# Unsplit fp32 products for most chunks, both branch projections among them, and another order in the second block

## The chip, the cores and the metric

The kernel runs on one NeuronCore of a Trainium2 chip. The metric is device time in microseconds (us) from launch to end, as the median of several runs. The engines are TensorE (PE in the profile, with its weight loads as PEld), VectorE (DVE), ScalarE (ACT), GpSimd (POOL) and SyncE (SP, whose queue issues most of the loads). Work is bound together by semaphores; each engine executes its own list of instructions in order.

## The reference, cut to what matters

A sequence of 256 tokens with 1024 features goes through two blocks in fp32. The change touches the second block alone:

```python
h = _rmsnorm(x, norm_mix_g)
proj = h @ w_in                       # r, k, v, the conv's input (glu), two gates
rkv = rkv + (_token_shift(rkv) - rkv) * mu_rkv
a_out = _rwkv7_mixer(h, r, k, v, ...)     # recurrence over tokens, 16 heads of 64
c_out = _conformer_conv_mixer(glu_in, ...)  # u * sigmoid, 31-tap conv per feature, layer norm, silu
gates = sigmoid(gate_logits).reshape(b, t, 2, 1024)
merged = gates[:, :, 0] * (a_out @ w_rwkv_proj) + gates[:, :, 1] * (c_out @ w_conv_proj)
x = x + merged @ w_out
x = x + square(relu(_rmsnorm(x, norm_ff_g) @ w_ff1)) @ w_ff2
```

## The kernel before

Activations of the second block stand feature-first: eight tiles of 128 features by 256 tokens. Weights come from HBM in **chunks** of 512 output features, each chunk in four pieces of 512 KB (256 input features by 512 outputs). A piece is loaded into `raw` by the SP queue (`fetch`, a ring of three slots).

Most products are **split products** (`feat`, line 266). `split` (lines 238 and 239) makes two tiles of a piece: `whi`, rounded to the matmul's short fp32 form by ACT, and `wlo`, the remainder, by DVE. The activations have been split in the same way (`xh`, `xl`). A 128x128 weight block then takes three matmuls, hi by hi, hi by lo and lo by hi: 96 matmuls of 256 columns for a chunk. `whi` and `wlo` have three slots each (`streams("s2", 3, 3)`). The output projection and the feed-forward (`toks`, line 284, and `feat`) take the same slots. Only `gated` (line 1586, the projection of the conv branch) multiplies **unsplit** fp32 weights, 32 products for a chunk, straight from tiles `wd`, which it places in the slots of `whi` and `wlo`.

The string `PROG` lists the steps of the second block's middle: K and R are the r, k, v products of the first and second half of the heads (three chunks each), L the low-rank products, A the preparation of a half's recurrence (norms by a `rsqrt` of ten DVE instructions), B its block matrices `G` with a small triangular solve on DVE whose data go through HBM (`blka`, `sy`, `blkb`, `T0T`), M the five pipelined steps of a half's recurrence over its chunks of tokens (chains of 64x64 matmuls with evictions between them; each step depends on the last), O the normalisation of its output into `y`, U the conv's input (two chunks each, half of the features), C one feature tile of the 31-tap convolution (`conv_tile`, 30 DVE instructions of line 1454, called taps here, after one ACT instruction), G a chunk of gates, S the layer norm of the conv's output, D the `gated` projection of a chunk of the conv branch. `merge2` follows: it splits `y` into hi and lo, multiplies it by `w_rwp` as a split product, merges, and multiplies by `w_o2`.

A planner turns this list into one order for each engine: it takes the instructions that are ready and lets later steps fill the waits of earlier ones; a step marked "!" keeps its first matmul or tap at its place in the list. So a step's instructions stand mingled with those of its neighbours, and matmuls of a chunk that stand in a recurrence's chain are called fillers here.

Of the kernel before, what the change touches and what calls it, by code (L numbers as in the profile page):

```python
# [167 lines left out]
class Net:  # L168
# [87 lines left out]
    def feat(self, xh, xl, src, n=4, tag="A", pieces=None, pin=lambda i: None):  # L256

        nc = self.nc
        out = [self.bank((128, 256), tag) for _ in range(n)]
        for k0, kn, hi, lo in (self.pieces(src, 128 * n) if pieces is None else pieces):  # L260
            for f in range(n):
                c = slice(f * 128, f * 128 + 128)
                for k in range(kn):
                    kt = k0 + k
                    for j, (w, x) in enumerate(((hi, xh), (hi, xl), (lo, xh))):
                        pin(nc.tensor.matmul(out[f], w[:, k, c], x[:, kt, :], start=(kt == 0 and j == 0),  # L266
                                             stop=(kt == 7 and j == 2)))
        return out
# [78 lines left out]
    def diag(self, r, n=2):  # L347

        out = []
        for tt in range(n):  # L350
            d = self.tmp.tile([128, 128], F32, name=self.name("dg"), tag="dg", bufs=2)
            self.nc.vector.tensor_scalar(d, self.ident, r[:, tt:tt + 1], None, op0=ALU.mult)
            out.append(d)
        return out

    def transpose_chunk(self, X, c, xh, xl, wcol=None, dg=None):


        nc = self.nc
        for fp in range(2 * c, 2 * c + 2):  # L360
            ps = self.bank((128, 2, 256), "B")
            for f in range(2):
                ft = 2 * fp + f
                for tt in range(2):
                    o, x = ps[:, f, tt * 128:tt * 128 + 128], X[:, tt, ft * 128:ft * 128 + 128]
                    if dg is None:
                        nc.tensor.transpose(o, x, self.ident)
                    else:
                        nc.tensor.matmul(o, x, dg[tt], start=True, stop=True)
            if wcol is None:  # L370
# [678 lines left out]
    def ple(self):  # L1049
        nc, a = self.nc, self.a  # L1050
        V, PE, S = nc.vector, nc.tensor, nc.scalar
        X2 = self.X2
        xh, xl = self.a8(F32R, s="xh"), self.a8(F32R, s="xl")
        for c in range(2):
            self.transpose_chunk(X2, c, xh, xl, "plw")
        s2 = self.small((128, 2), s="s2")
        V.tensor_reduce(s2, self.ss2, axis=AX.X, op=ALU.add)
        r = self.rstd_of(s2)
        self.ple_proj()
        wrow = self.act.tile([128, 1024], F32, name="wrow2", tag="row")  # L1060
        nc.gpsimd.dma_start(wrow, a["rows"][0])

        xw = self.a8(shape=(128, 2, 1024), s="xw")
        sa = self.small((128, 2, 2, 2), s="sa")
        for c in range(2):
            s = slice(512 * c, 512 * c + 512)
            for tt, ps in enumerate(self.toks(xh, xl, a["w_pg"][c])):
                g = self.t2(s="g")
                S.activation(g, ps, AF.Sigmoid, scale=r[:, tt:tt + 1])
                V.tensor_mul(g, g, self.U[:, tt, s])  # L1070
                V.tensor_add(X2[:, tt, s], X2[:, tt, s], g)
                self.square_sum(X2[:, tt, s], sa[:, 0, tt, c:c + 1])
# [12 lines left out]
        for c in range(2):  # L1085
            self.transpose_chunk(xw, c, *self.x2, "mixw", dg)
        self.rsqrt(v1, r1, t)
        for tt in range(2):
            nc.gpsimd.tensor_scalar(xw[:, tt, :], xw[:, tt, :], r1[:, tt:tt + 1], 1.0, op0=ALU.mult, op1=ALU.mult)
        self.xs = nc.dram_tensor("x_mid", (128, 2, 1024), F32).ap()  # L1090
        nc.gpsimd.dma_start(self.xs, xw)
# [354 lines left out]
    def conv_tile(self, up, ft, pin):  # L1446
# [35 lines left out]
    def mix2(self, late):  # L1482
        nc, a = self.nc, self.a
        V, PE, S, G = nc.vector, nc.tensor, nc.scalar, nc.gpsimd
        keep = self.keep
        xh, xl = self.x2
        self.y = y = self.cst.tile([128, 8, 256], F32, name="y", tag="xp")
        up = keep.tile([128, 8, 286], F32, name="up")
        with self.work("wkv", 1, 1):
            gates = self.branches(xh, xl, y, up)  # L1490
        self.tap("y", y)
        x4 = late.enter_context(self.pool("x4", 1, side="right"))
        self.x4 = [x4.tile([128, 8, 256], F32R, name=m) for m in ("h4", "l4")]
        with self.pool("post") as post:
            self.merge2(y, gates, post)

    def branches(self, xh, xl, y, up):
        nc, a = self.nc, self.a
        V, G = nc.vector, nc.gpsimd
        self.const2 = self.act.tile([128, a["const2"].shape[1]], F32, name="const2", tag="const2")  # L1500
# [12 lines left out]
        k0, k1, gates, st = {}, {}, {}, [{}, {}]  # L1513
        for tok in PROG.split():
            pin = self.pin(tok.endswith("!"))
            op, arg = tok[0], [int(x) for x in tok[1:].rstrip("!")]
            n = arg[0] if arg else 0
            if op == "L":
                self.lor = self.loras(xh, xl)
            elif op == "K":  # L1520
                k0[n] = self.rkv(xh, xl, n, 0, pin)
            elif op == "R":
                k1[n] = self.rkv(xh, xl, n, 1, pin)
            elif op == "U":
                self.glu(xh, xl, up, n, pin)
            elif op == "C":
                self.conv_tile(up, n, pin)
            elif op == "G":
                gates[n] = self.gate(xh, xl, n, pin)
            elif op == "S":  # L1530
                self.conformer(up, pin)
            elif op == "D":
                self.gated(gates[2 + n], up[:, :, 30:286], a["w_cvp"][n], pin)
            else:
# [37 lines left out]
        for f, ps in enumerate(self.feat(xh, xl, a["w_glu"][c])):  # L1572
            V.tensor_mul(up[:, 4 * c + f, 30:286], ps, sg[:, f, :])

    def gated(self, gt, z, w, pin):

        nc = self.nc
        out = [self.bank((128, 256), "A") for _ in range(4)]
        for p in range(4):
            pool, tag = ((self.wsp, "whi"), (self.wsp, "wlo"))[p % 2]  # L1580
            r = pool.tile([128, 2, 512], F32, name=self.name("wd"), tag=tag)
            nc.sync.dma_start(r, w[p])
            for f in range(4):
                for k in range(2):
# [3 lines left out]
        for f in range(4):  # L1588
            nc.vector.tensor_mul(gt[:, f, :], out[f], gt[:, f, :])

    def merge2(self, y, gates, post):
        nc, a = self.nc, self.a
        V, S, G = nc.vector, nc.scalar, nc.gpsimd
        yh, yl, mh, ml = (post.tile([128, 8, 256], F32R, name=n) for n in ("yh", "yl", "mh2", "ml2"))
        self.split_act(y, yh, yl, V)
        for c in range(2):
            for f, ps in enumerate(self.feat(yh, yl, a["w_rwp"][c])):
                m = self.t2((128, 256), s="m")
                V.tensor_mul(m, ps, gates[c][:, f])
                V.tensor_add(m, m, gates[2 + c][:, f])  # L1600
                S.activation(mh[:, 4 * c + f, :], m, AF.Copy)
                V.tensor_sub(ml[:, 4 * c + f, :], m, mh[:, 4 * c + f, :].bitcast(F32))
# [69 lines left out]


PROG1 = "X0 X1 T Z0 Z1 W D0 D1 Y5 Y6 Y0 Y1 Y2 v1 r Y3 Y4 Y7 N q0 q1 R0 k0 S k1 R1 v0 B1 A0 P12 A1 A2 B0 A3 A4 A5 A6 A7 P6 C0 C1"
PROG = "K0 L K2 K1 A0 U0 B0 U1 M0 M0 M0 M0 M0 O0 R0 R1 R2 A1 G0 B1 G2 M1 M1 M1 M1 G1 G3 M1 C0 C1 C2 C3 C4 C5 C6 C7 O1 S D1 D0"
STEPS = "m0 p0,m1 p1 s0,m2 p2 s1,m3 p3 s2,s3"
NEARLY = 12
NFIRST = 38
# [3 lines left out]
def net(ctx, tc, a, off, tap=None, upto=99):  # L1682
# [9 lines left out]
                n.mix1()  # L1692
                n.moe()
    late = ctx.enter_context(ExitStack())
    with n.streams("s2", 3, 3):
        with n.pool("keep") as n.keep:
            n.x2 = [n.keep.tile([128, 8, 256], F32R, name=m, tag=m) for m in ("xh2", "xl2")]
            with n.work("p3", 5):
                n.ple()
            n.mix2(late)  # L1700
# [19 lines left out]
```

## Time and profile before

| | |
|---|---|
| median of 3 runs | 1257.74 us (1257.6 to 1259.7) |
| the profiled execution | 1260.09 us |
| its span | 1258.4 us |
| mean granted TensorE clock | 0.955 |
| PE busy | 1131.2 us, 90% of the span |
| DVE busy | 745.1 us, 59% |
| ACT busy | 511.5 us, 41% |

The second block's middle runs from about 621 us (first product of K0) to about 1043 us (end of the product with `w_rwp`); the output projection takes until about 1070 us, the feed-forward until about 1247 us. The shares above are means over very different stages, so the stretches are to be read one by one: how much of a stretch PE is busy, at which granted clock (1.00 is 2.4 GHz, 0.50 is 1.2 GHz, a mean in between is a mixture of the two), and how busy DVE is at the same time.

### The profile page before, as it was taken

What the parts mean: (1) busy time and instruction counts of PE and PEld (TensorE: products, weight loads), DVE (VectorE), ACT (ScalarE), POOL (GpSimd) and SP (SyncE); (2) the same over time, 40 slices, a digit from 0 to 9 for tenths busy, and PEclk for the clock granted to TensorE, in tenths of its full rate; (3) what the DMA queues carried; (4) which work ended last, traced back from release to release, by engine and by line L of the source; (5) the groups of instructions that cost most, each with busy time, mean ns of one, the idle gap of its engine ahead of it and who ended that gap; (6) DMA issues with size and microseconds to landing.
All of it is one profiled execution on the core that took longest, in us unless ns stands there. A gap on an engine that the chain in (4) does not pass through costs nothing.

```text
span 1258.4 us, 20687 instructions
## 1 busy us (share of the span) xinstructions
PE 1131.2 (90%) x8211; PEld 887.1 (70%) x8211; DVE 745.1 (59%) x1513; ACT 511.5 (41%) x881; POOL 119.7 (10%) x126
## 2 busy tenths in 40 slices
PE   5999999999979988878789899998749999999996
PEld 5988976667754433216687798887736797999995
DVE  4777677656532111106846799889884366656555
ACT  4643644544411000006536535556215335545453
POOL 0002330001000000000200501014200000000000
PEclk9999999999979999998889899998857999999998
DMA  8743555327769999994353365122420136555552
GB/s 300 277 162 104 155 179 167 120 98 288 272 258 409 409 409 409 409 408 146 116 184 132 98 183 157 52 93 84 150 60 2 35 108 233 179 189 191 189 187 99
DMA packets 82981, 242.26 MB, mean 193 GB/s; under 512 B 24160, under 2 KB 24416, under 8 KB 82496
## 3 DMA queue, kind: packets, MB, share of 16 engines
q1 hardware_dynamic: 80224, 231.11, 51.3%
q0 software_dynamic: 2224, 8.90, 2.6%
q8 instruction: 66, 1.08, 0.4%
q10 hardware_dynamic: 432, 0.89, 0.2%
q14 instruction: 35, 0.29, 0.1%
HBM read 234.31 MB, written 4.46 MB: 190 GB/s over the span
## 4 chain that ended last, share of the span: by engine, by line
PE 47%; DVE 11%; DMA 5%; ACT 3%; issue 2%; POOL 1%; DVEq 0%; ACTq 0%; POOLq 0%; SPq 0%
PE ps L266 17%; PE acc L284 7%; DVE cv L1454 4%; PE ps L986 3%; PE ps L1007 3%; DMA we<-in_w_gu 3%; PE ps L284 2%; DVE wlo L239 2%; PE ps L1586 2%; PE ps L955 2%; DMA we<-in_w_dn 2%; PE acc L1015 2%; PE ps L1304 1%; ACT whi L238 1%; PE ps L1045 1%
## 5 line engine op out<-in xcount | busy, mean ns | idle before, releaser
L239 DVE TENSOR_TENSOR wlo<-raw,whi 128x1024 fp32r<-128x1024 f32 (+1 forms) x230 | 291.7, 1272 | 157.9 <-ACT whi L238 155.9
L238 ACT ACTIVATE whi<-raw 128x1024 fp32r<-128x1024 f32 (+1 forms) x230 | 242.2, 1055 | 289.7 <-PE ps L266 141.4
L266 PE MATMUL ps<-xh,whi 128*128 128x256 f32 x760 | 222.7, 293 | 9.1 <-DVE rkv L1135 4.2
L266 PE MATMUL ps<-xh,wlo 128*128 128x256 f32 x760 | 219.6, 291 | 1.6 <-DVE wlo L239 1.6
L266 PE MATMUL ps<-xl,whi 128*128 128x256 f32 x760 | 220.8, 291 | 0.0
L266 PEld LDWEIGHTS ps<-xh,whi 128*128 128x128 f32 x760 | 149.2, 196 | 14.7 <-DVE rkv L1135 4.7
L266 PEld LDWEIGHTS ps<-xh,wlo 128*128 128x128 f32 x760 | 148.4, 196 | 4.6 <-issue 1.8
L266 PEld LDWEIGHTS ps<-xl,whi 128*128 128x128 f32 x760 | 149.4, 197 | 3.1 <-issue 2.3
L1454 DVE SCALAR_TENSOR_TENSOR cv<-up,par,cv 128x256 f32<-128x256 f32 x232 | 106.3, 498 | 0.6
L986 PE MATMUL ps<-we,xg 128*32 128x512 f32 x512 | 75.9, 597 | 4.8 <-DMA we<-in_w_gu 4.8
L266 PE MATMUL ps<-h,whi 128*128 128x256 f32 x256 | 72.2, 282 | 0.0
L266 PE MATMUL ps<-l,whi 128*128 128x256 f32 x256 | 71.9, 281 | 0.0
L266 PE MATMUL ps<-h,wlo 128*128 128x256 f32 x256 | 71.9, 281 | 0.0
L284 PE MATMUL ps<-wlo,xh 128*128 128x512 f32 x128 | 50.7, 397 | 1.8 <-DVE wlo L239 1.8
L284 PE MATMUL ps<-whi,xh 128*128 128x512 f32 x128 | 50.9, 398 | 0.0
L284 PE MATMUL ps<-whi,xl 128*128 128x512 f32 x128 | 50.5, 394 | 0.0
L284 PE MATMUL acc<-wlo,fh 128*128 128x512 f32 x128 | 49.9, 390 | 0.0
L284 PE MATMUL acc<-whi,fl 128*128 128x512 f32 x128 | 49.9, 390 | 0.0
L284 PE MATMUL acc<-whi,fh 128*128 128x512 f32 x128 | 49.8, 389 | 0.0
L1007 PE MATMUL ps<-we,gT 128*32 128x512 f32 x256 | 44.1, 600 | 6.2 <-DVE gT L1001 3.5
L986 PEld LDWEIGHTS ps<-we,xg 128*32 128x32 f32 x512 | 16.4, 109 | 46.6 <-issue 24.8
L266 PEld LDWEIGHTS ps<-h,whi 128*128 128x128 f32 x256 | 48.2, 188 | 0.6 <-ACT re L1634 0.2
(477 smaller groups left out, 2025.2 us busy)
## 6 DMA issues: line engine op xcount, KB each, us to landing
we<-in_w_gu SPq DMA_DIRECT2D x128, 512.0 KB, 10.2
we<-in_w_dn SPq DMA_DIRECT2D x64, 512.0 KB, 10.2
raw<-in_w_ff SPq DMA_DIRECT2D x64, 512.0 KB, 4.2
raw<-in_w_g SPq DMA_DIRECT2D x32, 512.0 KB, 3.2
raw<-in_w_qkv SPq DMA_DIRECT2D x24, 512.0 KB, 3.2
raw<-in_w_rkv SPq DMA_DIRECT2D x24, 512.0 KB, 3.3
raw<-in_w_o SPq DMA_DIRECT2D x16, 512.0 KB, 5.8
raw<-in_w_glu SPq DMA_DIRECT2D x16, 512.0 KB, 3.2
```

The costliest lines, as they stand in the source:

```text
L238: nc.scalar.activation(hi, r, AF.Copy)
L239: nc.vector.tensor_sub(lo, r, hi.bitcast(F32))
L266: pin(nc.tensor.matmul(out[f], w[:, k, c], x[:, kt, :], start=(kt == 0 and j == 0), stop=(kt == 7 and j == 2)))
L284: pin(nc.tensor.matmul(out[tt], x[:, x0 + k, s], w[:, k, :], start=(kt == 0 and j == 0), stop=(kt == last and j == 2)))
L955: PE.matmul(ps[:, f, :], X1[:, tt, ft * 128:ft * 128 + 128], Pm[:, tt, :], start=(tt == 0), stop=(tt == 1))
L986: PE.matmul(gu[32 * e:32 * e + 32, :], xg[:, kt, 32 * e:32 * e + 32], w[e // 2][:, e % 2, :], start=(kt == 0), stop=(kt == 7), skip_group_ ...
L1007: PE.matmul(py[h][32 * e:32 * e + 32, :], gT[:, kt * 128 + 32 * e:kt * 128 + 32 * e + 32], w[e // 2][:, e % 2, :], start=(kt == 0), stop=( ...
L1015: PE.matmul(acc[tt][h], PT[:, tt * 128:tt * 128 + 128], y, start=False, stop=(q == 7 and n == 1), skip_group_check=True)
L1045: PE.matmul(ps, x[:, kt, ts], ww[:, kt, :], start=(n == 0), stop=(n == 5))
L1304: PE.matmul(ps[H(h), q, :], lhs[H(h), q, :], r, start=True, stop=True)
L1454: pin(nc.vector.scalar_tensor_tensor(last, x[:, j:j + 256], self.P("cw", 8 * j + ft), o, op0=ALU.mult, op1=ALU.add))
L1586: pin(nc.tensor.matmul(out[f], r[:, k, 128 * f:128 * f + 128], z[:, kt, :], start=(kt == 0), stop=(kt == 7)))
```

## The change

1. `feat` gets a second form: with `xl=None` it takes the loaded pieces as they are and makes one fp32 matmul where the split form makes three. The new tokens with "f" use it with `x32`, an unsplit copy of the activations: R0, R1, R2, U0, U1 (two chunks each) and G0 to G3.
2. `transpose_chunk` writes `x32` too, by eight more ACT instructions at the end of the first block. It takes 8 KB of each partition, and `wsp` now has two slots each for `whi` and `wlo` instead of three.
3. The product with `w_rwp` leaves `merge2` and becomes the steps W0 and W1, made by `gated` with unsplit weights; `y` is no longer split.
4. `PROG` is another list: the second half's products R, and its A, come ahead of the first half's recurrence, U0 after them; conv tiles are placed between the steps of both recurrences; W0 and W1 stand around S, ahead of D0 and D1. `diag` gets a third slot. (`conv_sum`, a conv on PE, is defined but no token calls it.)

So 13 chunks change form: three R, four U, four G and two W. K0 to K2 and L stay split, as do `w_o2` and the feed-forward.

```diff
     def feat(self, xh, xl, src, n=4, tag="A", pieces=None, pin=lambda i: None):
...
         out = [self.bank((128, 256), tag) for _ in range(n)]
+        if xl is None:
+            for p in range(4):
+                r = self.fetch(src[p])
+                for f in range(n):
+                    for k in range(2):
+                        kt = 2 * p + k
+                        pin(nc.tensor.matmul(out[f], r[:, k, f * 128:f * 128 + 128], xh[:, kt, :], start=(kt == 0),
+                                             stop=(kt == 7)))
+            return out
...
+                if x32 is not None:
+                    nc.scalar.activation(x32[:, ft, :], ps[:, f, :], AF.Copy, scale=self.P(wcol, ft))
...
+            xs = (x32, None) if "f" in tok else (xh, xl)
...
+            elif op == "W":
+                self.gated(gates[n], y, a["w_rwp"][n], pin)
...
-        yh, yl, mh, ml = (post.tile([128, 8, 256], F32R, name=n) for n in ("yh", "yl", "mh2", "ml2"))
-        self.split_act(y, yh, yl, V)
+        mh, ml = (post.tile([128, 8, 256], F32R, name=n) for n in ("mh2", "ml2"))
         for c in range(2):
-            for f, ps in enumerate(self.feat(yh, yl, a["w_rwp"][c])):
-                m = self.t2((128, 256), s="m")
-                V.tensor_mul(m, ps, gates[c][:, f])
+            for f in range(4):
+                m = gates[c][:, f]
                 V.tensor_add(m, m, gates[2 + c][:, f])
...
-PROG = "K0 L K2 K1 A0 U0 B0 U1 M0 M0 M0 M0 M0 O0 R0 R1 R2 A1 G0 B1 G2 M1 M1 M1 M1 G1 G3 M1 C0 C1 C2 C3 C4 C5 C6 C7 O1 S D1 D0"
+PROG = "K0 K2 L K1 A0 R0f R1f R2f B0 A1 U0f M0 C0 M0 M0 C1 G1f M0 M0 B1 O0 C2 U1f M1 C3! G0f M1 C6 M1 G3f M1 M1 C4! G2f C5 C7! O1 W0 S W1 D0 D1"
...
-    with n.streams("s2", 3, 3):
+    with n.streams("s2", 3, 2):
```

How the order moves shows at three places. In the rows below a line number of the new kernel is 9 to 27 higher than that of the same statement before (266 became 275 for split products, 1304 became 1315, 1312 became 1323, 1454 became 1465, 377 became 386).

On PE, the second half's recurrence begins. Before:

```order
L1304 MATMUL ps_8111<-const_82,T0T 64x64 x8
L1304 MATMUL ps_8121<-T_1473_8105,LT_8104 64x64 x8
L1304 MATMUL ps_8131<-T_1474_8106,T0T 64x64 x8
L1304 MATMUL ps_8141<-T0T,T_1474_8106 64x64 x8
L1319 MATMUL ps_8151<-T_1476_8108,G_7871 32x32 x8
L1327 MATMUL ps_8162<-T_1475_8107,T_1474_8106 32x32
```

In the new kernel, at the same place, where line 266 is now the unsplit product (`x` is `x32`, and the weights are the raw tile):

```order
L1315 MATMUL ps_7447<-const_82,T0T 64x64 x8
L266 MATMUL ps_7580<-x_4807,raw_7602 128x256 x2
L1315 MATMUL ps_7457<-T_1395_7441,LT_7440 64x64 x8
L266 MATMUL ps_7581<-x_4807,raw_7602 128x256 x2
L1315 MATMUL ps_7467<-T_1396_7442,T0T 64x64 x8
L1315 MATMUL ps_7477<-T0T,T_1396_7442 64x64 x8
L266 MATMUL ps_7578<-x_4807,raw_7612 128x256
L1330 MATMUL ps_7487<-T_1398_7444,G_7109 32x32 x8
```

Gate products now stand between the links of the chain, where before link followed on link: 59 unsplit products are spread over this recurrence.

On DVE, the same recurrence; `cv` and the last `up` of a tile are the convolution's taps, `T` the chain's evictions, and "x16" is a run of sixteen. Before:

```order
L1454 SCALAR_TENSOR_TENSOR cv_9150<-up,par,cv_9150 128x256
L1454 SCALAR_TENSOR_TENSOR cv_9182<-up,par,cv_9182 128x256
L1454 SCALAR_TENSOR_TENSOR up<-up,par,cv_9150 128x256
L1454 SCALAR_TENSOR_TENSOR cv_9182<-up,par,cv_9182 128x256 x16
L1312 TENSOR_TENSOR T_1476_8108<-ps_8131,T_1473_8105 128x256
L1313 TENSOR_TENSOR T_1475_8107<-ps_8141,T0T 128x256
L1454 SCALAR_TENSOR_TENSOR cv_9182<-up,par,cv_9182 128x256 x4
L1454 SCALAR_TENSOR_TENSOR up<-up,par,cv_9182 128x256
L1466 TENSOR_SCALAR mean_9319<-ps_9310 128x256
```

In the new kernel:

```order
L1465 SCALAR_TENSOR_TENSOR cv_7763<-up,par,cv_7763 128x256
L1323 TENSOR_TENSOR T_1398_7444<-ps_7467,T_1395_7441 128x256
L1465 SCALAR_TENSOR_TENSOR cv_7763<-up,par,cv_7763 128x256
L1324 TENSOR_TENSOR T_1397_7443<-ps_7477,T0T 128x256
L1465 SCALAR_TENSOR_TENSOR cv_7545<-up,par,cv_7545 128x256
L1465 SCALAR_TENSOR_TENSOR cv_7763<-up,par,cv_7763 128x256
L1465 SCALAR_TENSOR_TENSOR cv_7545<-up,par,cv_7545 128x256
```

Before, the convolution is nearly over when the second recurrence begins. Now 86 of its 240 taps stand in the first recurrence, 101 in the second, and a run of 27 behind the second's last eviction.

On ACT, the end of the first block, where the activations of the second are written (`xh` and, in the new kernel, `x`, which is `x32`), and the first halves of weights after them. Before:

```order
L377 ACTIVATE xh_4805<-ps_5149,par 128x256
L377 ACTIVATE xh_4805<-ps_5140,par 128x256
L377 ACTIVATE xh_4805<-ps_5149,par 128x256
L238 ACTIVATE whi_5288<-raw_5286 128x1024
L238 ACTIVATE whi_5336<-wl_5330 128x1024
```

In the new kernel:

```order
L386 ACTIVATE xh_4805<-ps_5156,par 128x256
L390 ACTIVATE x_4807<-ps_5145,par 128x256
L390 ACTIVATE x_4807<-ps_5156,par 128x256
L386 ACTIVATE xh_4805<-ps_5156,par 128x256
L238 ACTIVATE whi_5267<-raw_5265 128x1024
L390 ACTIVATE x_4807<-ps_5156,par 128x256
L238 ACTIVATE whi_5297<-raw_5295 128x1024
L238 ACTIVATE whi_5341<-raw_5339 128x1024
```

The eight writes of `x32` stand between those of `xh`, one of them even behind the next piece's `whi`; and the pieces that follow are now K2's (`raw`), where L's scaled weights (`wl`) stood.

## Rows read from the trace of the kernel before

**Rows 1.** Part 1 of the page: busy time, share of the span, instructions of an engine.

```profile
PE 1131.2 (90%) x8211; PEld 887.1 (70%) x8211; DVE 745.1 (59%) x1513; ACT 511.5 (41%) x881; POOL 119.7 (10%) x126
```

**Rows 2.** Windows: length, busy (instructions) of PE, PEld, DVE, ACT, POOL; clock, DMA share, GB/s.

```profile
621.00:675.00 54.00, 49.79 (x390) 49.35 (x389) 29.96 (x50) 24.11 (x36) 8.75 (x11) 0.94 0.56 183
675.00:711.00 36.00, 29.08 (x184) 22.77 (x183) 30.10 (x54) 23.87 (x39) 15.44 (x15) 0.95 0.24 80
711.00:727.00 16.00, 15.42 (x118) 14.11 (x119) 10.40 (x15) 4.30 (x6) 8.28 (x7) 0.79 0.43 137
727.00:771.00 44.00, 43.23 (x356) 42.32 (x355) 43.41 (x107) 18.80 (x24) 0.00 (x0) 1.00 0.70 197
771.00:823.00 52.00, 51.38 (x936) 43.64 (x937) 43.98 (x97) 28.74 (x72) 4.52 (x5) 1.00 0.19 63
823.00:892.00 69.00, 63.31 (x402) 52.43 (x401) 61.17 (x120) 35.38 (x61) 26.72 (x28) 0.90 0.26 88
892.00:934.00 42.00, 21.28 (x163) 18.61 (x160) 41.52 (x118) 6.02 (x11) 0.21 (x1) 0.74 0.51 144
934.00:991.00 57.00, 52.41 (x835) 40.52 (x836) 22.50 (x54) 26.10 (x72) 3.46 (x5) 0.80 0.04 11
991.00:1021.00 30.00, 29.46 (x135) 23.27 (x134) 16.36 (x34) 9.79 (x17) 4.81 (x7) 1.00 0.16 54
1021.00:1043.00 22.00, 22.00 (x193) 21.84 (x193) 13.67 (x23) 8.77 (x11) 1.14 (x2) 1.00 0.56 183
```

**Rows 3.** The chain that ended last, in order of time, from 880 to 1043 us.

```profile
901.04 6.16 DVE cv L1454 x16
...
1009.32 12.09 PE ps L1586 x56
1021.41 21.63 PE ps L266 x189
```

**Rows 4.** Waits, 621 to 1043 us: engine, line, releaser; total, times, longest.

```profile
PE ps L1464 <- DVE up L1454: 19.0, 2, 12.0
```

**Rows 5.** Part 5 of the page: splitting and taps; busy us, mean ns, idle before.

```profile
L239 DVE TENSOR_TENSOR wlo<-raw,whi 128x1024 fp32r<-128x1024 f32 (+1 forms) x230 | 291.7, 1272 | 157.9 <-ACT whi L238 155.9
...
L1454 DVE SCALAR_TENSOR_TENSOR cv<-up,par,cv 128x256 f32<-128x256 f32 x232 | 106.3, 498 | 0.6
```

**Rows 6.** Tile `wd`, the unsplit products: duration ns minimum, median, maximum; first, last start.

```profile
L1586 PE MATMUL ps<-up,wd x128: 377/378/484, 971.8 to 1021.0; 128*128 128x256 f32 x128
```

**Rows 7.** A 20-us window at the start of the second recurrence.

```profile
920.00:940.00 20.00, 7.81 (x104) 6.03 (x106) 19.32 (x48) 1.30 (x4) 1.53 (x2) 0.50 0.21 34
```

**Rows 8.** DVE's groups of taps in the first and the second recurrence (771:823, 934:991).

```profile
L1454 DVE SCALAR_TENSOR_TENSOR cv<-up,par,cv 128x256 f32<-128x256 f32 x65 | 28.0, 491 | 0.0
```

```profile
L1454 DVE SCALAR_TENSOR_TENSOR cv<-up,par,cv 128x256 f32<-128x256 f32 x9 | 5.0, 560 | 0.3
```

**Rows 9.** ACT's timeline at the end of the first block: start, us, operation.

```profile
620.30 1.74 ACT L377 ACTIVATE xh<-ps,par 128x256 fp32r<-128x256 f32 x4 [0.42 <-PE ps L369]
```

**Rows 10.** The chain that ended last, from 618 to 690 us, in L.

```profile
627.82 6.54 DMA raw<-in_w_l
```

**Rows 11.** DMA issues, 675 to 960 us: KB each, median us to landing.

```profile
blka<-G SPq DMA_DIRECT2D x4, 256.0 KB, 4.2
T0T<-blkb SPq DMA_DIRECT2D x4, 256.0 KB, 4.4
...
sy<-blka SPq DMA_DIRECT2D x2, 128.0 KB, 4.7
blkb<-W SPq DMA_DIRECT2D x2, 128.0 KB, 3.2
```

**Rows 12.** Timelines of ACT and DVE in the feed-forward: start, us, idle before, releaser.

```profile
1150.93 1.06 ACT L238 ACTIVATE whi<-raw 128x1024 fp32r<-128x1024 f32 x1 [1.89 <-PE ps L266]
1153.77 1.06 ACT L238 ACTIVATE whi<-raw 128x1024 fp32r<-128x1024 f32 x1 [1.78 <-PE ps L266]
```

```profile
1152.03 1.23 DVE L239 TENSOR_TENSOR wlo<-raw,whi 128x1024 fp32r<-128x1024 f32 x1 [1.72 <-ACT whi L238]
```

More of the change, by code (lines that the diff above doesn't have):

```diff
@@ L350, in diag @@
         for tt in range(n):
-            d = self.tmp.tile([128, 128], F32, name=self.name("dg"), tag="dg", bufs=2)
+            d = self.tmp.tile([128, 128], F32, name=self.name("dg"), tag="dg", bufs=3)
             self.nc.vector.tensor_scalar(d, self.ident, r[:, tt:tt + 1], None, op0=ALU.mult)
@@ L354, in diag, with transpose_chunk @@
         return out
-    def transpose_chunk(self, X, c, xh, xl, wcol=None, dg=None):
+    def transpose_chunk(self, X, c, xh, xl, wcol=None, dg=None, x32=None):
         nc = self.nc
@@ L1085, in ple @@
         for c in range(2):
-            self.transpose_chunk(xw, c, *self.x2, "mixw", dg)
+            self.transpose_chunk(xw, c, *self.x2[:2], "mixw", dg, self.x2[2])
         self.rsqrt(v1, r1, t)
@@ L1455, in conv_tile, with conv_sum @@
                                                op1=ALU.add))
+    def conv_sum(self, up, ft, pin):
+        nc = self.nc
+        x = up[:, ft, :]
+        ps = self.bank((128, 256), "A")
+        for j in range(31):
+            d = self.tmp.tile([128, 128], F32, name=self.name("dg"), tag="dg", bufs=3)
+            nc.scalar.activation(d, self.ident, AF.Copy, scale=self.P("cw", 8 * j + ft))
+            pin(nc.tensor.matmul(ps, d, x[:, j:j + 256], start=(j == 0), stop=(j == 30)))
+        nc.scalar.activation(x[:, 30:286], ps, AF.Identity, bias=self.P("cb", ft))
     def conformer(self, up, pin):
@@ L1485, in mix2 @@
         keep = self.keep
-        xh, xl = self.x2
+        xh, xl, x32 = self.x2
         self.y = y = self.cst.tile([128, 8, 256], F32, name="y", tag="xp")
@@ L1489, in mix2 @@
         with self.work("wkv", 1, 1):
-            gates = self.branches(xh, xl, y, up)
+            gates = self.branches(xh, xl, x32, y, up)
         self.tap("y", y)
@@ L1494, in mix2, with branches @@
         with self.pool("post") as post:
-            self.merge2(y, gates, post)
-    def branches(self, xh, xl, y, up):
+            self.merge2(gates, post)
+    def branches(self, xh, xl, x32, y, up):
         nc, a = self.nc, self.a
@@ L1515, in branches @@
             pin = self.pin(tok.endswith("!"))
-            op, arg = tok[0], [int(x) for x in tok[1:].rstrip("!")]
+            xs = (x32, None) if "f" in tok else (xh, xl)
+            op, arg = tok[0], [int(x) for x in tok[1:].rstrip("!f")]
             n = arg[0] if arg else 0
@@ L1520, in branches @@
             elif op == "K":
-                k0[n] = self.rkv(xh, xl, n, 0, pin)
+                k0[n] = self.rkv(*xs, n, 0, pin)
             elif op == "R":
-                k1[n] = self.rkv(xh, xl, n, 1, pin)
+                k1[n] = self.rkv(*xs, n, 1, pin)
             elif op == "U":
-                self.glu(xh, xl, up, n, pin)
+                self.glu(*xs, up, n, pin)
             elif op == "C":
                 self.conv_tile(up, n, pin)
+            elif op == "E":
+                self.conv_sum(up, n, pin)
             elif op == "G":
-                gates[n] = self.gate(xh, xl, n, pin)
+                gates[n] = self.gate(*xs, n, pin)
             elif op == "S":
                 self.conformer(up, pin)
+            elif op == "W":
+                self.gated(gates[n], y, a["w_rwp"][n], pin)
             elif op == "D":
@@ L1573, in glu, with gated @@
             V.tensor_mul(up[:, 4 * c + f, 30:286], ps, sg[:, f, :])
-    def gated(self, gt, z, w, pin):
+    def gated(self, gt, z, w, pin, tag="A"):
         nc = self.nc
-        out = [self.bank((128, 256), "A") for _ in range(4)]
+        out = [self.bank((128, 256), tag) for _ in range(4)]
         for p in range(4):
-            pool, tag = ((self.wsp, "whi"), (self.wsp, "wlo"))[p % 2]
-            r = pool.tile([128, 2, 512], F32, name=self.name("wd"), tag=tag)
+            pool, t = ((self.wsp, "whi"), (self.wsp, "wlo"))[p % 2]
+            r = pool.tile([128, 2, 512], F32, name=self.name("wd"), tag=t)
             nc.sync.dma_start(r, w[p])
@@ L1589, in gated, with merge2 @@
             nc.vector.tensor_mul(gt[:, f, :], out[f], gt[:, f, :])
-    def merge2(self, y, gates, post):
+    def merge2(self, gates, post):
         nc, a = self.nc, self.a
         V, S, G = nc.vector, nc.scalar, nc.gpsimd
-        yh, yl, mh, ml = (post.tile([128, 8, 256], F32R, name=n) for n in ("yh", "yl", "mh2", "ml2"))
-        self.split_act(y, yh, yl, V)
+        mh, ml = (post.tile([128, 8, 256], F32R, name=n) for n in ("mh2", "ml2"))
         for c in range(2):
-            for f, ps in enumerate(self.feat(yh, yl, a["w_rwp"][c])):
-                m = self.t2((128, 256), s="m")
-                V.tensor_mul(m, ps, gates[c][:, f])
+            for f in range(4):
+                m = gates[c][:, f]
                 V.tensor_add(m, m, gates[2 + c][:, f])
@@ L1694, in net @@
     late = ctx.enter_context(ExitStack())
-    with n.streams("s2", 3, 3):
+    with n.streams("s2", 3, 2):
         with n.pool("keep") as n.keep:
-            n.x2 = [n.keep.tile([128, 8, 256], F32R, name=m, tag=m) for m in ("xh2", "xl2")]
+            n.x2 = [n.keep.tile([128, 8, 256], F32 if m == "x32" else F32R, name=m, tag=m) for m in ("xh2", "xl2", "x32")]
             with n.work("p3", 5):
```

## The prediction

> **What bounds the kernel now.** Part 1 of the page has PE busy for 90% of the span [rows 1], which reads like a full engine; the mean hides the second block's middle. So the windows come next [rows 2]: 621 to 1043 us cut at the stages. In each the reader is to work out what PE loses: the idle time, plus the busy time times (1 - clock), since at a mean granted clock of 0.80 a fifth of the busy time is waiting in another form. In order of rows: 4.2 + 3.0 = 7.2; 6.9 + 1.5 = 8.4; 0.6 + 3.2 = 3.8; 0.8; 0.6; 5.7 + 6.3 = 12.0; 20.7 + 5.5 = 26.2; 4.6 + 10.5 = 15.1; 0.5; 0. The sum is 74.6 of 422 us. Half of it lies between 892 and 991 us.
>
> Why there, the other columns tell. From 892 to 934 us DVE is busy 41.5 of 42 us while PE idles for half, and the chain of waits runs through taps of the convolution [rows 3]; PE's longest wait is for a conv tile, 19.0 us [rows 4]. DVE is late because it carries the weight splits, 1.27 us each, beside the taps [rows 5]. When the second recurrence follows, PE has nothing else left: the clock, 0.50 just before [rows 7], comes back only in part and is 0.80 over that stretch. In the first recurrence, with about 150 split matmuls as fillers, PE is busy 51.4 of 52 us at clock 1.00 [rows 2]. So in this middle PE's work bounds some stages and DVE others.
>
> **What the change adds: dearer products.** A run of 189 split matmuls took 21.63 us, 0.114 us each [rows 3]; in the feed-forward a piece of 24 takes 1153.77 - 1150.93 = 2.84 us, 0.118 each [rows 12]. So the 96 of a chunk take 11.0 to 11.4 us; I take 11.2. Unsplit products show in D: 12.09 us for 56 records [rows 3], and each product leaves two records (128 for 64 products [rows 6]), so 0.432 us a product and 13.8 us for a chunk of 32. That is 2.6 us more, 34 us for 13 chunks, all on PE; the bounds are 2.4 and 2.8, 31 to 37 us.
>
> The record says nothing of how the hardware makes such a product. The Trainium skill (FP8 and Floating Point Precision, TensorE Precision Notes) gives a true fp32 product as four passes through the array. Against three split matmuls that alone would make a chunk 11.2 x 4/3 = 14.9 us (an estimate by that page), and 13 of them 49 us more, 15 us worse than my sum (the last rival below). The D row, which has the very form that is added, says 13.8, and goes into the sum.
>
> **What it removes: DVE and ACT work.** 13 chunks of four pieces lose their split: 52 x 1.27 = 66 us of DVE [rows 5]. The 240 taps stay, at 6.16 / 16 = 0.385 us each in a row [rows 3]. Off PE's path nothing of this counts by itself; it counts by the taps coming earlier, and by chunks whose matmuls wait for no DVE at all. With the taps beside the recurrences the conv-bound stretch at 892 to 934 us should be gone. The loss by stage that I expect:
>
> - K0 to K1: 8 us (7.2 before). The wait for L's weights, 6.5 us in the chain [rows 10], falls away as K2 stands between. Against that, the `x32` writes: one costs 1.74 / 4 = 0.435 us [rows 9], eight are 3.5 us on ACT, about half ahead of the last `xh`; and two slots instead of three let a split start only when the piece two before is done. Bounds 4 and 13.
> - A0 and B0: 7 (8.4 + 3.8 before). The `rsqrt` chain is the same length, but the R products that fill it no longer wait for `wlo` behind that chain on DVE.
> - Up to the first recurrence: 1.5 (0.8). The way of the solve through HBM, 4.2 + 4.7 + 3.2 + 4.4 = 16.5 us of landings [rows 11] and the solve between them, lies beside 44 unsplit products, 19 us, and all of A1. SP issues U0's pieces between these transfers; five pieces are ahead, and no piece is needed before its turn.
> - First recurrence: 1 (0.6). 48 products, 20.7 us, replace some 150 split matmuls, 17.5 (counts from the two orders), so it lasts about 55 us. DVE has 86 taps there, where it had 65 [rows 8] and six splits: 33 against 25 + 7.6.
> - B1 and O0: 3 (12.0). About 64 products, 27 us, and O0 cover the second solve.
> - The conv-bound stretch: 0 (26.2).
> - Second recurrence: 3 (15.1). 59 products, 25.5 us, keep the clock up as in the first. DVE gets 101 taps, 39 us, where it had 9 [rows 8]; with the chain's own work, 44.0 - 28.0 - 6 x 1.27 = 8 us in the first recurrence [rows 2, 5, 8], that fits into the 60 us that PE needs.
> - O1: 6 (0.5 for O1 and D together). Here 27 taps, 10.4 us, stand on DVE ahead of O1's `rsqrt`. PE has G2's last 17 products, 7.3 us, and the half of W0 that needs only the first half's `y`, 6.9 us, to lie over them; the last normalisations, one after the other through ACT, POOL and DVE, are not covered.
> - W0's rest, S, W1, D0, D1: 2. W1's 13.8 us lie over the layer norm's chain.
>
> That is 31.5 us against 74.6: 43 gone. W0's four loads stand on SP ahead of R0's last piece and wait for K1's slots; they are hidden as long as PE is in A0 then; without that cover R0's last piece would come a landing later, some 4 us as for the loads of [rows 11]. The eight multiplications by gates move from `merge2` to W, and the split of `y` goes; both lay beside products. `merge2` itself loses a product's wait between its parts; I take 2 us less for it, between 0 and 4.
>
> **Two slots in the feed-forward.** This is the one edit outside the middle. The row of before shows a piece every 2.84 us, with `whi` starting as a piece ends (1150.93, 1153.77) and `wlo` ending at 1152.03 + 1.23 = 1153.26, 2.33 us after [rows 12]. With three slots that is a piece early. With two, the same split must be there when the next piece is through, 2.84 us after, and `wlo` only for the third matmul: 0.5 to 0.75 us of room. I take 0 us; the bad end is below.
>
> **Sum.** 34 - 43 - 2 = -11. PE's busy time also counts the tail of a small matmul in which a filler could run; the recurrences' 51.4 and 52.4 us [rows 2] hold some of it, so I take 2 us more: **-13** from the 1260.09 us of the profiled execution, 1247. The median of before lies 2.35 us under its profiled run, so the forecast for the median is **1245 us**.
>
> **The rivals.**
>
> *More than that* (18%). Fillers without any need of DVE let PE run nearly full from R0 on, and half of the remaining 31.5 us goes as well: 1245 - 15 = 1230. For it: 727 to 823 us, where PE has fillers, loses 1.4 of 96 us [rows 2]. Against it: the chain of O1 has no fillers left but W0's half.
>
> *The waits only move* (14%). In the second recurrence DVE's taps (39 us, at the 0.50 us that a record lasts [rows 5] rather 50) delay the chain's evictions, then the 27 taps delay O1 in full; 8 + 5 us come back, and 1245 + 12 = 1257, no change to be measured. A second form of it is the clock: it was 0.50 at PE's 7.8 busy of 20 us [rows 7], and 0.80 after. If one or two products between links don't bring it back, the 10.5 us stay, 1255. The Trainium skill (TensorE: Matmul & The Clock Gate, What's actually happening) has the low rate as the default, which activity lifts; by that, recurrences with fillers run at full clock. The first recurrence, at 1.00 with fillers, agrees.
>
> *Slower: two slots don't carry the feed-forward* (11%). Its place is `wlo` of each of the 64 pieces, behind the hidden layer's evictions on ACT and DVE. The room is 0.5 to 0.75 us a piece; each delay beyond it is PE's. From 0.2 us a piece the gain is gone (64 x 0.2 = 13); at 0.3 the time is 1245 + 19 = 1264. Against it: ACT idles 1.8 us before each `whi` of the row [rows 12].
>
> *Slower: the product is dearer than D shows* (7%). If a product costs four split matmuls, 0.467 us, and not the 0.432 of D [rows 3], a chunk takes 14.9 us and the change adds 49 us, not 34: 1245 + 15 = 1260. It decides from 0.464 us on. D's row speaks against it, but in D the weights lay ready; in the fillers raw pieces land just in time.
>
> **How the numbers follow.** My forecast (1236 to 1254) has 50%, the four rivals 18, 14, 11 and 7%. A measurement of this kernel can tell about 0.2%, 2.5 us: faster means below 1255.2. The forecast, the first rival and a third of the second give 0.73 faster; the rest of the second 0.09 the same; the last two 0.18 slower. The range for 8 in 10 runs from the larger gain (1228, with the cheaper end of the products) to 1264.
>
> **What would show it.** In the windows: PE busy near the full length from R0 to the end of the second recurrence, clock 1.00 in both, no stretch of taps alone; a chunk's unsplit run at 13.8 us; PE's wait for `up` by taps gone. The forecast is wrong if the feed-forward gets longer by more than 5 us, if K0 to K1 lasts over 60 us, or if PE waits in O1 for over 10 us.

## The result and the profile after

The changed kernel takes 1243.35 us (median; 1241.48 to 1243.91), the kernel before 1257.93 us in the same comparison: a ratio of 0.9879, with a 95% interval of 0.9862 to 0.9896. That is 14.6 us less; 1245 us had been forecast. The profiled execution went from 1260.09 to 1243.91 us.

The windows of the changed kernel, cut at its own stages (length; busy time of PE, PEld, DVE, ACT, POOL with instructions; granted clock; DMA share; GB/s), answer to [rows 2]:

```profile
620.50:671.30 50.80, 48.45 (x385) 46.50 (x384) 30.51 (x54) 25.03 (x41) 8.67 (x11) 1.00 0.57 191
671.30:701.00 29.70, 22.93 (x102) 15.60 (x102) 23.62 (x50) 16.08 (x31) 13.38 (x15) 0.99 0.39 139
701.00:733.00 32.00, 31.82 (x146) 27.41 (x148) 5.07 (x13) 4.25 (x9) 2.47 (x3) 0.90 0.36 115
733.00:766.00 33.00, 30.92 (x172) 25.30 (x170) 19.14 (x58) 9.02 (x18) 5.92 (x7) 1.00 0.64 159
766.00:789.00 23.00, 21.23 (x138) 13.97 (x138) 19.78 (x42) 11.40 (x22) 12.84 (x14) 0.78 0.18 60
789.00:841.00 52.00, 51.77 (x812) 39.23 (x812) 41.65 (x99) 20.07 (x56) 2.88 (x4) 0.93 0.16 52
841.00:897.00 56.00, 54.92 (x412) 43.02 (x410) 39.93 (x109) 13.92 (x36) 9.65 (x15) 1.00 0.43 113
897.00:955.00 58.00, 57.79 (x808) 44.64 (x803) 49.41 (x114) 18.70 (x53) 2.23 (x3) 1.00 0.23 74
955.00:987.00 32.00, 30.34 (x138) 23.75 (x137) 18.27 (x46) 9.17 (x22) 5.03 (x9) 1.00 0.31 99
987.00:1028.60 41.60, 41.60 (x194) 36.46 (x193) 17.16 (x43) 8.81 (x17) 0.00 (x0) 1.00 0.34 114
```

The rows are, in order: K0 to K1; A0; R; U0 and the start of A1; the rest of A1; the first recurrence; B1, O0 and U1; the second recurrence; O1 with S; W1, D0 and D1 with the rest of W0. Read as before the change (idle time plus busy time times one minus the clock) PE loses 2.4, 7.0, 3.4, 2.1, 6.4, 3.9, 1.1, 0.2, 1.7 and 0 us, 28.2 in all, where the kernel before lost 74.6. The stretch in which DVE ran taps alone is gone. The second recurrence, at 0.80 before, has PE busy 57.8 of 58 us at clock 1.00. That 0.80 was no steady level: in the kernel before, the clock stood at 0.50 from 915 us to the end of this row,

```profile
950.00:955.00 5.00, 5.00 (x48) 3.22 (x49) 0.00 (x0) 3.44 (x12) 0.00 (x0) 0.50 0.00 0
```

and at 1.00 from 960 us to the end of the stage.

What was paid for it stands in the chain of waits that ended last (start, us, what), which answers to [rows 3]; these pieces are whole runs:

```profile
671.24 0.93 PE ps L1237 x4
...
897.42 1.06 PE ps L266 x4
...
987.18 41.44 PE ps L1613 x192
1028.62 11.23 PE ps L293 x49
...
1087.43 11.36 PE ps L275 x96
1098.79 10.93 PE acc L293 x48
```

The 192 records of W and D are 96 unsplit products, 41.44 / 96 = 0.432 us each, 13.81 us a chunk. A chunk of split products in the feed-forward still takes 11.36 us. K1 ends at 671.2 us. The products ahead of the output projection end at 1028.6, where they ended at 1043 before [rows 3]. The feed-forward's pieces take as long as with three slots; in the kernel before they were:

```profile
1103.61 11.36 PE ps L266 x96
1114.96 10.93 PE acc L284 x48
```

PE's wait for a conv tile [rows 4] is no longer in the list of PE's waits (621 to 1029 us); what leads it there is:

```profile
PE ps L266 <- issue: 5.3, 1, 5.3
PE ps L1330 <- DVE T L1323: 2.2, 2, 1.6
PE ps L1246 <- DVE iv L304: 2.1, 1, 2.1
```

On part 5 of the page the splitting is down by 52 pieces and 66 us, and the taps are as many and as long as before [rows 5]:

```profile
L239 DVE TENSOR_TENSOR wlo<-raw,whi 128x1024 fp32r<-128x1024 f32 (+1 forms) x178 | 225.7, 1272 | 149.9 <-ACT whi L238 144.8
...
L1465 DVE SCALAR_TENSOR_TENSOR cv<-up,par,cv 128x256 f32<-128x256 f32 x232 | 107.6, 500 | 2.6
```

### The profile page after: what moved, and what is told of

Read it like the earlier page. It is cut to its first block, busy times and chain, and to the rows that moved or that the text cites. A ratio compares the mean times of both kernels' runs of the same rounds, so it can differ in the third digit from the quotient of the medians.

```text
span 1242.2 us, 19656 instructions
## 1 busy us (share of the span) xinstructions
PE 1146.0 (92%) x7795; PEld 873.9 (70%) x7795; DVE 693.8 (56%) x1459; ACT 461.4 (37%) x835; POOL 109.7 (9%) x126
## 4 chain that ended last, share of the span: by engine, by line
PE 51%; DMA 8%; DVE 6%; ACT 2%; issue 1%; POOL 1%; DVEq 0%; ACTq 0%; SPq 0%; POOLq 0%
PE ps L266 12%; PE ps L275 9%; PE acc L293 7%; DMA we<-in_w_gu 5%; PE ps L1613 4%; PE ps L293 3%; PE ps L997 3%; DMA we<-in_w_dn 2%; PE ps L966 2%; PE ps L1018 2%; PE ps L1315 1%; DVE cv L1465 1%; PE acc L1026 1%; ACT whi L238 1%; PE ps L1056 1%
## 5 line engine op out<-in xcount | busy, mean ns | idle before, releaser
L239 DVE TENSOR_TENSOR wlo<-raw,whi 128x1024 fp32r<-128x1024 f32 (+1 forms) x178 | 225.7, 1272 | 149.9 <-ACT whi L238 144.8
L238 ACT ACTIVATE whi<-raw 128x1024 fp32r<-128x1024 f32 (+1 forms) x178 | 187.6, 1055 | 221.3 <-PE ps L275 78.6
L266 PE MATMUL ps<-x,raw 128*128 128x256 f32 x704 | 179.8, 402 | 5.3 <-issue 5.3
L266 PEld LDWEIGHTS ps<-x,raw 128*128 128x128 f32 x704 | 132.3, 196 | 30.9 <-issue 10.6
L275 PE MATMUL ps<-xh,whi 128*128 128x256 f32 x408 | 116.7, 287 | 4.4 <-ACT cv L446 1.5
L275 PE MATMUL ps<-xl,whi 128*128 128x256 f32 x408 | 115.1, 283 | 0.0
L275 PE MATMUL ps<-xh,wlo 128*128 128x256 f32 x408 | 114.2, 285 | 0.9 <-DVE wlo L239 0.8
L275 PEld LDWEIGHTS ps<-xh,whi 128*128 128x128 f32 x408 | 78.0, 191 | 6.8 <-ACT whi L238 3.4
L275 PEld LDWEIGHTS ps<-xh,wlo 128*128 128x128 f32 x408 | 77.1, 191 | 2.1 <-DVE wlo L239 1.7
L275 PEld LDWEIGHTS ps<-xl,whi 128*128 128x128 f32 x408 | 78.1, 191 | 0.0
```

The costliest lines, as they stand in the source:

```text
L238: nc.scalar.activation(hi, r, AF.Copy)
L239: nc.vector.tensor_sub(lo, r, hi.bitcast(F32))
L266: pin(nc.tensor.matmul(out[f], r[:, k, f * 128:f * 128 + 128], xh[:, kt, :], start=(kt == 0), stop=(kt == 7)))
```

## The experiments

The theory: the unsplit form costs PE time and is worth it only where DVE has no time for splits; the new order needs that DVE time for its taps. So neither of the two should bring the gain alone. Both runs that part them keep `x32`, two slots and the unsplit W steps, so these are no gain by themselves either. The main rivals: the order did it and the form only costs; or the form did it and the order is a detail. Ratios below are to the kernel before, run on the same chip as the experiment; chips differed, with before at 1257.2 to 1259.9 us.

**The order alone.**

```diff
-PROG = "... A0 R0f R1f R2f B0 A1 U0f M0 C0 M0 M0 C1 G1f ... U1f ... G0f ... G3f ... G2f ..."
+PROG = "... A0 R0 R1 R2 B0 A1 U0 M0 C0 M0 M0 C1 G1 ... U1 ... G0 ... G3 ... G2 ..."
```

> The changed kernel with its new list of steps, x32, two slots and the W steps, but with R, U and G (11 chunks) as split products again; so the order without the form. Theory (the form is paid for by DVE time: 44 splits of 1.27 us = 56 us more on DVE): PE's own work is 11 x 2.6 = 29 us less, but the taps come later (67 of 240 instead of 27 stand behind the second recurrence's last eviction, 15 us more of DVE ahead of O1), so it gives back most: 1243 to 1256. Rival (the order alone did it, the form only costs PE time): 1243 - 29 = 1214 to 1222.

Measured: 1263.13 us, ratio 1.0054 (1.0032 to 1.0075): slower than before, and slower than I expected. Read from windows of 40 us as above, PE loses 78 us in the middle, 74.6 before. The chain of waits behind the second recurrence (start, us, what) has the taps:

```profile
952.64 21.38 DVE cv L1465 x54
```

and PE's largest wait (total, times, longest) is for the end of a norm chain (the ten DVE steps of a `rsqrt`):

```profile
PE ps L1246 <- DVE iv L304: 23.0, 4, 10.6
```

Two of its four waits are long (timeline of PE: start, us, operation, idle before):

```profile
773.45 1.22 PE L1246 MATMUL ps<-iv,const 32*128 32x256 f32 x4 [8.24 <-DVE iv L304]
979.66 1.22 PE L1246 MATMUL ps<-iv,const 32*128 32x256 f32 x4 [10.56 <-DVE iv L304]
```

The later one, ahead of O1, comes from the run of 54 taps with O1's own chain behind it; the late taps were foreseen. The earlier one, in A1, was not. There taps, and no splits, stand between the steps, and PE's products over the chain end 2.3 us after it begins; in the changed kernel U0's longer products last 6.4 us into it, and the wait is 2.1 us. The first recurrence then runs in part at the lower clock, which is the costliest stretch of this run:

```profile
780.00:820.00 40.00, 29.76 (x490) 25.23 (x490) 34.43 (x66) 15.83 (x43) 15.81 (x17) 0.60 0.08 28
```

The rival (1214 to 1222) falls.

**The form alone.**

```diff
-PROG = "K0 K2 L K1 A0 R0f R1f R2f B0 A1 U0f M0 C0 ..."
+PROG = "K0 L K2 K1 A0 U0f B0 U1f M0 M0 M0 M0 M0 O0 R0f R1f R2f A1 G0f B1 G2f M1 M1 M1 M1 G1f G3f M1 C0 C1 C2 C3 C4 C5 C6 C7 O1 W0 W1 S D1 D0"
```

> The changed kernel with the list of steps of before, and in it R, U, G unsplit and W0 W1 after O1; so the form without the order. Theory (both are needed: form frees DVE, order puts fillers into the second recurrence): the stretch bound by taps (26 us lost) goes, 34 us of dearer products come, the second recurrence stays without fillers at a lowered clock (15 us lost): 1255 to 1265, about the time before. Rival (the form alone, DVE's freedom, brings the gain): 1241 to 1247.

Measured: 1260.54 us, ratio 1.0022 (1.0006 to 1.0039), the time that the theory has. Its place for the loss is wrong. The second recurrence (906 to 964 us) was expected without fillers at a lowered clock; it has 49 unsplit products between its links, of G and W0, and runs at 1.00. PE loses elsewhere (windows, columns as above):

```profile
820.00:860.00 40.00, 35.95 (x151) 26.25 (x150) 38.52 (x90) 15.77 (x29) 10.92 (x15) 0.88 0.25 86
860.00:900.00 40.00, 37.47 (x194) 31.65 (x194) 27.59 (x70) 7.81 (x15) 12.24 (x14) 0.91 0.42 113
900.00:940.00 40.00, 38.84 (x552) 29.41 (x552) 2.90 (x7) 13.98 (x41) 3.25 (x5) 1.00 0.32 92
940.00:980.00 40.00, 34.95 (x437) 25.19 (x431) 11.81 (x29) 12.43 (x35) 2.84 (x6) 0.91 0.13 41
980.00:1020.00 40.00, 32.36 (x139) 27.46 (x138) 15.10 (x39) 8.77 (x18) 2.17 (x4) 0.93 0.30 92
```

DVE is nearly idle in the second recurrence, and nothing uses that time. The first two rows hold A1 and the second solve, the last two the recurrence's end, O1 and S, and in these four PE loses 32 of its 45 us. So the form alone takes the loss from 74.6 to 45 us and pays 32 us of dearer products for it; the new order, with the form, takes it on to 28.2. Form and order are each worth nothing or less; together they are worth 1.2%.

**DVE's time taken away, under both forms.** The same edit was made in the run with the order alone and in the changed kernel.

```diff
-        for j in range(1, 31):
+        for j in range(2, 31, 2):
```

> The run with the order alone (R, U and G split, 1263 us) with 15 of the convolution's 30 added taps left out of each feature tile, the odd ones but the first; so that part of the convolution is not computed. It takes 8 x 15 x 0.385 = 46 us from DVE and nothing from PE. Theory (DVE's time alone is what the split form lacks under the new order): the run of 54 taps after the second recurrence (21 us in the chain) halves, the norm chains wait less, and PE's 29 us of cheaper products show: 1222 to 1240. Rival (the split form itself delays PE, by its slots, by ACT, by each piece's two steps): 1250 to 1262.

> The changed kernel with the same 15 taps of each tile left out. Theory (in the changed kernel DVE no longer bounds the recurrences; PE is busy 57.8 of 58 us in the second): little, from 3 to 6 us by the taps ahead of O1 and those that the first links of both recurrences wait for: 1237 to 1241. Rival (taps still set the recurrences' pace, DVE busy 49 of 58 us): 46 us less DVE give 10 us or more, below 1234.

Measured: with split products 1243.29 us, ratio 0.9877 (0.9855 to 0.9899), 1.8% below the run with all taps; with unsplit ones 1245.91 us, ratio 0.9888 (0.9862 to 0.9915), no change against 0.9879. So 46 us of DVE work are worth some 22 us under the order with split products, and nothing in the changed kernel, where I had expected 3 to 6. The first is a little over the expected range, and this row, to be read beside the 23.0 above, says where:

```profile
PE ps L1246 <- DVE iv L304: 11.6, 3, 8.2
```

The wait ahead of O1 is gone with the taps; the one in A1 is as long as with all of them:

```profile
774.59 1.22 PE L1246 MATMUL ps<-iv,const 32*128 32x256 f32 x4 [8.25 <-DVE iv L304]
```

The pair shows that DVE's time is most of what the split form lacked, and that in the changed kernel DVE, busy 49 of 58 us in the second recurrence, does not set its pace. What is left in A1 is, by the traces, PE's cover: the split products are over too soon. No run parts that from the rest.

**Split products again in one place at a time.** First the gates of the second recurrence, where DVE is busiest:

```diff
-... M1 C3! G0f M1 C6 M1 G3f M1 M1 C4! G2f C5 C7! O1 ...
+... M1 C3! G0 M1 C6 M1 G3 M1 M1 C4! G2 C5 C7! O1 ...
```

> The changed kernel with G0, G3 and G2 as split products (R, U, G1 and W unsplit). These chunks stand in and behind the second recurrence, where DVE is busy 49 of 58 us. Theory (the form is worth its price where DVE has no time): PE gets 3 x 2.6 = 7.8 us less, DVE 12 x 1.27 = 15 us more just there, 64 us for a stretch of 58, and as many taps behind the last eviction; so no gain but a loss, 1245 to 1254. Rival (DVE has enough time, PE's work alone counts): 1236 to 1239.

Measured: 1252.07 us, ratio 0.9943 (0.9927 to 0.996), 8 us slower than the changed kernel. In its chain the taps stand again, and O1's norm chain comes late:

```profile
944.57 18.21 DVE cv L1465 x46
```

```profile
PE ps L1246 <- DVE iv L304: 13.6, 2, 11.6
```

Three chunks, some 7 us less of PE work (3 x 2.45), and a loss. Then R, where DVE is busy 5 of 32 us (third row of the windows above):

```diff
-... A0 R0f R1f R2f B0 ...
+... A0 R0 R1 R2 B0 ...
```

> The changed kernel with the three R chunks as split products (the other eight unsplit). There DVE is busy 5 of 32 us (701 to 733 us of the changed kernel), so by the theory that the form matters only where DVE has no time, splitting is free here and PE gets 3 x 2.6 = 7.8 us less: 1235 to 1238. Rival (split products wait for DVE's norm chain of A0 and for the two slots, also held by W0's weights): 1243 to 1250.

Measured: 1240.03 us, ratio 0.9872 (0.9843 to 0.9901). The profiled span is 5.0 us shorter (1237.2 against 1242.2) and the medians differ by 3, but by the ratios it is 0.9 us, and the intervals overlap: no loss, and a gain that is not shown. With U1 split as well:

```diff
-... O0 C2 U1f M1 ...
+... O0 C2 U1 M1 ...
```

> The changed kernel with R and U1 as split products; the run with R alone gave 1240. U1's first chunk stands beside the second solve, where DVE is free for most of the time, its second chunk at the start of the second recurrence. Theory (split where DVE is idle, unsplit where it is not): PE gets 5.2 us less, of which the first chunk's 2.6 count: 1236 to 1239. Rival (the splits stand on DVE ahead of the solve and of the first taps, which then come late): 1241 to 1247.

Measured: 1238.15 us, ratio 0.9833 (0.9816 to 0.9849). This beats both kernels; against the changed one it is 0.5% less, and the intervals do not meet. With U0 too:

```diff
-... B0 A1 U0f M0 ...
+... B0 A1 U0 M0 ...
```

> The changed kernel with R, U0 and U1 as split products; with R and U1 the ratio to before was 0.983. U0's products lie over the first solve's way through HBM. Theory: PE has 5.2 us less to do there, but no less to wait for, so the time stays within 2 us of the run with R and U1 split (ratio 0.982 to 0.985). Rival (PE's work counts there as well): 0.979 to 0.980.

Measured: median 1250.26 us, ratio 0.9932 (0.9912 to 0.9952), with one execution, the profiled, at 1240.69 us; that one's span, 1239.0 us, is 2 us over the run before. Neither expectation holds. In the profiled execution the first recurrence looks like this:

```profile
780.00:840.00 60.00, 47.08 (x829) 39.60 (x829) 51.01 (x107) 24.84 (x66) 12.19 (x13) 0.77 0.11 37
```

Here PE idles 13 of 60 us, and the clock is at 0.77; in the changed kernel the first recurrence has PE busy 51.8 of 52 us at 0.93. With U0's products shorter, G1's, which are the recurrence's fillers, stand ahead of it: four split matmuls and no unsplit product run beside its chain from 785 to 815 us, where the run with R and U1 split has 20 unsplit ones from 790 to 815. A run of 15 taps, too, now stands on DVE ahead of an eviction of the chain. The other four executions have a mean clock of 0.958 to 0.960 over the whole kernel, the profiled one 0.970; they have no trace, so that their 7 to 10 us are the clock's is likely and not shown.

**Two slots alone.**

```diff
-    with n.streams("s2", 3, 3):
+    with n.streams("s2", 3, 2):
```

> The kernel before with two slots instead of three for the split weights, nothing else. Theory: 0.5 to 0.75 us of room a piece is enough, 1257 to 1260. Rival (two slots stall the split pipeline): 64 pieces of the feed-forward at 0.3 us, 1277.

Measured: 1260.36 us, ratio 1.0018 (0.9998 to 1.0039); single executions lie between 1254.9 and 1262.9. At most 0.4%, not told apart from nothing, and far from the rival. The chain has the feed-forward's pieces as before (after the first, 11.36 and 10.93 us):

```profile
1077.82 16.68 PE ps L266 x137
1094.50 10.90 PE acc L284 x48
```

**K2 ahead of L**, once added to the kernel before and once taken from the changed one.

```diff
-PROG = "K0 L K2 K1 A0 U0 B0 ..."
+PROG = "K0 K2 L K1 A0 U0 B0 ..."
```

> The kernel before with K0 K2 L K1 instead of K0 L K2 K1, nothing else. Theory: the 6.5 us for L's weights in the chain go, PE's 4.2 us of idle time and the lower clock behind it with them, and K1 ends 3 to 5 us earlier; what stands behind is bound by DVE until 934 us, so little of it is left at the end: 1254 to 1258. Rival (the early stages set the end): 1252 to 1253.5.

Measured: 1251.07 us, ratio 0.9936 (0.992 to 0.9953), 8 us less; its profiled execution, 1255.5 us, is the slowest of its four, 4.6 us below the profiled one of before. The median is more than I or the rival had. The chain shows the whole middle moved:

```profile
647.88 23.73 PE ps L266 x195
671.61 0.58 PE ps L1226 x2
...
896.03 5.67 DVE cv L1454 x15
...
1005.14 12.09 PE ps L1586 x56
1017.23 21.97 PE ps L266 x192
```

K1 ends at 671.6 us, 3.3 us earlier; the run of taps on which the middle hangs begins at 896.0 where it began at 901.0, and the product with `w_rwp` at 1017.2 where it began at 1021.4 [rows 3]. My reason for little (DVE bounds what follows) was wrong: DVE's work in the middle is fed by these products, so its bound moves forward with them. That is 4 to 5 us in the trace; the other 3 us of the median have no trace.

```diff
-PROG = "K0 K2 L K1 A0 R0f ..."
+PROG = "K0 L K2 K1 A0 R0f ..."
```

> The changed kernel with K0 L K2 K1 as before instead of K0 K2 L K1. Theory: the wait of PE behind L's weights (4.2 us idle and some 3 us at the lower clock in the kernel before, 2.4 us lost in this part of the changed one) comes back: 1247 to 1249. Rival (two slots and the writes of x32 set this part, not L's weights): 1242 to 1245.

Measured: 1246.05 us, ratio 0.9887 (0.986 to 0.9914), against 0.9879 with K2 first: 1 us, and the intervals overlap. In the traces the end of K1 goes from 671.24 to 673.14 us, but with K2 first it lies anywhere from 670.6 to 673.3 in the runs of this document. So in the changed kernel no worth of this swap is shown, where I had given it 4 to 6 us, though the wait itself is back:

```profile
628.36 6.46 DMA raw<-in_w_l
```

## Why the prediction was right

**The price of the form.** Forecast 13.8 us a chunk against 11.2; measured 13.81 against 11.36. So 13 chunks cost 13 x 2.45 = 32 us, in the lower half of the bounds 31 to 37. The rival with four split matmuls a product is out: W's rows show 0.432 us, and so does a run straight from `raw`, in the stretch B1, O0 and U1, where the rival feared pieces that land just in time:

```profile
848.05 17.27 PE ps L266 x80
```

Between the links of a recurrence two products take 1.06 us (row at 897.42), 0.53 each, but in the whole this adds nothing: taking the losses off the windows, PE's work is 347.4 us before and 379.9 now, 32.5 more.

**The loss by stage.** 31.5 us had been expected, 28.2 are left; but the stages miss on both sides, and the sum is better than its terms:

| stage | expected | measured |
|---|---|---|
| K0 to K1 | 8 | 2.4 |
| A0, B0 with R | 7 | 10.4 |
| up to the first recurrence | 1.5 | 8.5 |
| first recurrence | 1 | 3.9 |
| B1, O0 | 3 | 1.1 |
| second recurrence | 3 | 0.2 |
| O1 | 6 | 1.7 |
| W, S, D | 2 | 0 |

K0 to K1, below its bounds of 4 to 13: neither the writes of `x32` nor two slots cost what I gave them; the first split product of K0 starts at 620.44 us, where it started at about 621. The largest misses are the stage ahead of the first recurrence (7 us), K0 to K1 (6) and O1 (4). Ahead of the first recurrence I looked at the solve's transfers and took A1 for cover. A1 is itself a chain of small DVE steps, and PE idles 3.9 us beside it; the rest of the 8.5 is the clock, 0.78 in A1's last part, after a wait of 2.1 us for the norm chain. The chain of waits runs through these steps:

```profile
762.43 1.39 DVE iv L304
763.84 0.85 DVE vt L302
764.71 0.84 DVE vt L303
...
783.14 0.97 DVE BK L1203
784.14 0.84 DVE rkv L1206
785.33 0.85 DVE BK L1203
786.21 0.84 DVE rkv L1206
```

In O1 the products of W0's first half, and then S, did cover the last normalisations.

**The sum.** 32 - (74.6 - 28.2) = -14.4 us over the middle (the windows' lengths give -13.9), and 16.2 us between the two profiled executions; the rest lies outside the middle. The 2 us for `merge2` were wrong: from the last product of the middle to the first of the feed-forward it took 26.7 us and takes 27.2. The 2 us for overlapping records in the recurrences can't be told apart from the clock there. So the mechanism was right, with a price within 2 us; that the whole came within 2 us as well is partly luck, since the stages' misses cancel.

**The rivals.** More gain: the changed kernel did not take it, but the run with R and U1 split took a part, by cheaper products and not by shorter waits. The waits only move: the taps do not set the pace (half of them gone, no change), and the clock is 1.00 in the second recurrence; the first, in the run whose fillers were spent ahead of it, at 0.77, shows that the danger is real. Two slots: out; the feed-forward ran from 1070.1 to 1246.9 us and runs from 1055.9 to 1232.0. Two readings were wrong on the way: the 19.0 us of [rows 4] are two waits for conv tiles together, the longest is 12.0; and the clock in the second recurrence before came back in full, but late, by the row at 950.

**What was not seen** is how the gain divides. I had the form's DVE time and the order as one step. Alone, the form gives 1.0022 and the order 1.0054; swapping L and K2, which I had put at a few us that would partly be lost, is worth 0.6% by itself in the kernel before, half of the whole gain, and nothing that is shown in the changed one. And the form's own gift was taken for the order's: with the old order, too, the unsplit products became fillers of the second recurrence and kept its clock; the new order pays ahead of it and behind it.

## What to carry to other kernels

Where one engine prepares operands for another, price the preparation stage by stage: the same trade (three cheap products and a split, or one dear product and none) paid in the second recurrence, where DVE was full, and cost time beside R and U1, where DVE had time left. Price the cover too: U0 lay where DVE had time, and splitting it lost more than R and U1 had won; the one traced execution shows the recurrence's fillers spent early. Test a change of form and a change of order apart and together; here each was worth nothing without the other. A saving at the head of a stretch moves the engine that bounds the stretch too, if that engine is fed from there; being off PE's list of waits does not make it free.

## What the runs showed of the hardware

An unsplit 128x256 product took 0.432 us against 0.355 for three split matmuls (3 x 11.36 / 96), so it cost as much as 3.65 split matmuls. The four passes that the Trainium skill (FP8 and Floating Point Precision, TensorE Precision Notes) gives for true fp32 would be 0.473 us at the split matmul's pace, an estimate by that page; the measurement decides for 0.432 here.

And work that looks spare may hold up the clock. In the run with R, U0 and U1 split, PE is nearly idle for 5 us and then works at 0.50, through 810 us, with hardly a filler:

```profile
780.00:785.00 5.00, 1.23 (x8) 0.95 (x6) 5.00 (x8) 1.88 (x5) 3.69 (x4) 0.97 0.32 105
785.00:790.00 5.00, 2.79 (x34) 2.36 (x34) 4.96 (x12) 3.27 (x6) 2.17 (x3) 0.50 0.00 0
```

The 60 us around them had a mean clock of 0.77; with U0 unsplit the same window was:

```profile
780.00:840.00 60.00, 55.96 (x935) 44.62 (x930) 54.29 (x119) 25.35 (x66) 11.79 (x12) 0.97 0.19 63
```

This last row is of the run with R and U1 split. U0's form moved fillers, splits and taps together, so no run shows the idle time alone to be the cause.
